# Seven block products in place of eight for two of eight k-pairs of most gate/up column pairs

## The chip, the cores and the metric

The kernel runs on one core of one Trainium2 chip. The metric is the device time of one execution in microseconds (us), and less is better. Before the change the median of three runs is 1765.84 us (1765.79 to 1766.41). Differences within 0.2% of that, some 3.5 us, are treated as no change. All data is fp32 in memory. Each engine works through its own queue of instructions in order and waits at an instruction until the semaphores it names have been reached: TensorE (PE, with its weight loads PEld), VectorE (DVE), ScalarE (ACT), GpSimd (POOL), and SyncE (SP), which here only issues transfers.

## The reference

One decoder layer for 256 tokens of width 2048, with two gated feed-forward networks of inner width 5632 around a mixing layer (linear attention and dilated attention). What is computed, cut to what the change touches:

```
x = x + 0.5 * swiglu(rms_norm(x), w_gate1, w_up1, w_down1)
h = rms_norm(x);  z = h @ w_in;  ... attention ...;  x = x + concat(o_g, o_a) @ w_out
x = x + 0.5 * swiglu(rms_norm(x), w_gate2, w_up2, w_down2)

def swiglu(x, w_gate, w_up, w_down):
    return (silu(x @ w_gate) * (x @ w_up)) @ w_down
```

The change touches `x @ w_gate` and `x @ w_up` in both networks: (256 x 2048) times (2048 x 5632), twice each.

## The kernel before, in words

**Numbers.** TensorE takes its operands as two fp32r parts: a value is split into a high part and the rest. `split` (lines 87 to 90) makes both: ACT copies the source to the high part (line 89), then DVE subtracts it from the source (line 90). A product of two values is then three matmuls: high by high (line 211), high by low part of the weights (line 213), low part of the activations by high (line 215).

**Tiling.** Tokens are two tiles of 128 (`t`). The 2048 input features are 16 k-tiles of 128. The activations of all k-tiles, split, lie in `hh` and `hl`. A gate/up **column pair** is 512 columns of `w_gate` and the same 512 of `w_up`, and there are 11 of them (`b` = 0 to 10) in each network. For one column pair `column_pair` goes through the 16 k-tiles; for each it does both token tiles, both columns and three matmuls of 128x128 by 128x512, that is 12 matmuls, so 192 for a column pair. They accumulate in four PSUM banks `ps` (two token tiles by gate and up).

**Weights.** A `raw` tile holds 1 MB of weights: two k-tiles (a **k-pair**), gate and up. SP loads it (line 181) into one of three buffers; SP can issue the load for a buffer only after the last reader of the tile that lay there before. For each k-tile `prepare` makes a pair of tiles `wh` and `wl` (128x1024) by `split`; each has four buffers (`WBUF`), and ACT can write one only when TensorE has finished with the k-tile four places earlier. `weights` calls `prepare` so that two k-tiles beyond the present one have been asked for.

**Evacuation.** After the last k-tile of a token tile `evac` (lines 263 to 275) applies silu to the gate (ACT, line 265), multiplies by up (DVE, line 266), transposes 32x32 squares (DVE, line 104), moves the squares with 16 small transfers from POOL's queue (line 109) and appends to the list `later` a `finish` that splits the result into `uh` and `ul`, the input of the down projection. `later` is worked off between the k-tiles of the next column pair.

**Order.** The program is written as loops, and a scheduler then sets the order of each engine's queue. PSUM has eight banks: six for accumulators (`pacc`), two for transposes and attention (`ptp`).

Of the kernel before, what the change touches and what calls it, by code (L numbers as in the profile page):

```python
# [26 lines left out]
FT = FF // P  # L27
NT = S // P
EPS = 1e-6
WBUF = 4  # L30
WARM = 10
GH, GDK, GDV, RANK = 4, 128, 256, 16
AH, HD = 8, 128
# [3 lines left out]
def layer_kernel(tc, x, xT, gains, gla_gate_up, gla_gate_bias, gla_out_norm, att_q_norm, att_k_norm,  # L37
# [6 lines left out]
    with ExitStack() as es:  # L44
        cst = es.enter_context(tc.tile_pool(name="cst", bufs=1))
        wp = es.enter_context(tc.tile_pool(name="wp", bufs=2))
        pacc = es.enter_context(tc.tile_pool(name="pacc", bufs=6, space=PSUM))
        ptp = es.enter_context(tc.tile_pool(name="ptp", bufs=2, space=PSUM))

        def acc_bank():  # L50
            return pacc.tile([P, 512], F32, name="acc", tag="acc")

        def t512(name):
            return cst.tile([P, 512], F32, name=name, tag="t512", bufs=4)
# [1 line left out]
        def tp_bank():  # L56
            return ptp.tile([P, 512], F32, name="tp", tag="tp")
# [29 lines left out]
        def split(dst_h, dst_l, src):  # L87

            nc.scalar.activation(dst_h, src, AF.Copy)  # L89
            nc.vector.tensor_sub(dst_l, src, dst_h.bitcast(F32))  # L90
# [20 lines left out]
        def in_order(a):  # L111

            return a.rearrange("p (q j c) -> p j q c", q=4, j=4)

        def runs(a):
            return a.rearrange("p j (q c) -> p j q c", q=4)
# [26 lines left out]
            rsqrt(rt[:, t:t + 1], ssum[:, t:t + 1])  # L143


        jobs = [(w, i, k) for w in (w_ff1, w_dn1) for i in range(w.shape[0]) for k in range(2)]
        jobs += [(w_mix, i, k) for i in range(3 * KT // 2) for k in range(2)] + ["low"]
        jobs += [(w_mix, i, k) for i in range(3 * KT // 2, 3 * KT) for k in range(2)]
        jobs += [(w, i, k) for w in (w_out, w_ff2, w_dn2) for i in range(w.shape[0]) for k in range(2)]

        AHEAD = 2
        ready = []
# [3 lines left out]
        def wtile(name):  # L156
            return wp.tile([P, 2, 512], F32R, name=name, tag=name, bufs=WBUF)

        def prepare():
            if not jobs:  # L160
                return
            job = jobs.pop(0)
            if job == "low":
                raw = wp.tile([P, KT, P], F32, name="raw", tag="raw", bufs=3)
                nc.sync.dma_start(raw, w_low.rearrange("p (k f) -> p k f", f=P))
                got = []
                for i in range(2):
# [7 lines left out]
            if k == 0:  # L175
                raw = raws[0] = wp.tile([P, 2, 2, 512], F32, name="raw", tag="raw", bufs=3)
                flat = raw.rearrange("p k j f -> p (k j f)")
                parts = 1 if started else 4
                started.append(True)
                for c in range(0, 2048, 2048 // parts):  # L180
                    nc.sync.dma_start(flat[:, c:c + 2048 // parts], w[i, :, c:c + 2048 // parts])
            wh, wl = wtile("wh"), wtile("wl")
            if len(started) < 3:
                started.append(True)
                for j in range(2):
                    split(wh[:, j], wl[:, j], raws[0][:, k, j])
            else:
                split(wh, wl, raws[0][:, k])
            ready.append((wh, wl))
# [12 lines left out]
        def halves(a):  # L202
            return a.rearrange("p (b a) -> p b a", b=2)

        def products(ps, t, acts, ws, first, last, js=((0, 1),)):
            for jj in js:
                for i, ((ah, al, k), (wh, wl)) in enumerate(zip(acts, ws)):
                    sh = ah[:, k, t * P:(t + 1) * P]
                    sl = al[:, k, t * P:(t + 1) * P]
                    for j in jj:  # L210
                        nc.tensor.matmul(ps[j], lhsT=sh, rhs=alt(wh[:, j, :]), start=first and i == 0, stop=False)  # L211
                    for j in jj:
                        nc.tensor.matmul(ps[j], lhsT=sh, rhs=alt(wl[:, j, :]), start=False, stop=False)  # L213
                    for j in jj:
                        nc.tensor.matmul(ps[j], lhsT=sl, rhs=alt(wh[:, j, :]), start=False, stop=last and i == len(ws) - 1)  # L215
# [3 lines left out]
        def run_later(n):  # L219
            for _ in range(min(n, len(later))):  # L220
                later.pop(0)()

        def column_pair(acts, evac, span=28, due=None, extra=None, final=False):

            ps = [None] * NT
            n = len(acts)  # L230
            total = done = 0
            i = 0
            while i < n:
                if i == due:
                    done += len(later)
                    run_later(len(later))
                if extra and i in extra:
                    extra[i]()
                g = WBUF if final and i == n - WBUF else 1
                ws = [weights() for _ in range(g)]  # L240
                for t in range(NT):
                    step = 2 * i + t
                    total = max(total, done + len(later))
                    go = max(-(-total * min(step + 1, span) // span) - done, 0)
                    done += min(go, len(later))
                    run_later(go)
                    if i == 0:
                        ps[t] = [acc_bank(), acc_bank()]
                    last = i + g == n
                    products(ps[t], t, acts[i:i + g], ws, i == 0, last, ((0,), (1,)) if g > 1 else ((0, 1),))  # L250
                    if last:
                        evac(t, [b.rearrange("p (a b) -> p b a", b=2) for b in ps[t]])
                i += g
# [3 lines left out]

        def ffn(name, done, extra=None, final=False):
            with tc.tile_pool(name=name, bufs=1, reuse_waits="tile") as fp:
                uh = fp.tile([P, FT, S], F32R, name="uh")  # L260
                ul = fp.tile([P, FT, S], F32R, name="ul")
                for b in range(FF // 512):
                    def evac(t, ps, b=b):
                        sg, u = t512("sg"), t512("u")
                        nc.scalar.activation(halves(sg), ps[0], AF.Silu, scale=rt[:, t:t + 1])  # L265
                        nc.vector.scalar_tensor_tensor(halves(u), ps[1], rt[:, t:t + 1], halves(sg), op0=ALU.mult, op1=ALU.mult)  # L266

                        us = t512("us")
                        ur = fp.tile([P, 512], F32, name="ur", tag="ur", bufs=2)
                        squares(us, u)  # L270
                        move_squares(ur, us)

                        def finish():
                            split(*(runs(a[:, 4 * b:4 * b + 4, t * P:(t + 1) * P]) for a in (uh, ul)), in_order(ur))

                        later.extend([lambda: None] * (2 if t else 6) + [finish])
                    if b:
                        column_pair(hacts, evac)
                    else:
                        column_pair(hacts, evac, span=16, due=15 if extra else 8, extra=extra)  # L280
                for cp in range(2):
                    def evac(t, ps, cp=cp):
                        for j in range(2):
                            c = 2 * cp + j
                            blk = xs[:, t, c * 512:(c + 1) * 512]
                            nc.vector.scalar_tensor_tensor(halves(blk), ps[j], 0.5, halves(blk), op0=ALU.mult, op1=ALU.add)  # L286
                            done(t, c, blk)
                    column_pair([(uh, ul, k) for k in range(FT)], evac, span=28 + 32 * cp, final=final and cp == 1)


        xTv = xT.rearrange("(k p) s -> p k s", p=P)
# [412 lines left out]
```

## Time and profile before

| | |
|---|---|
| median of three runs | 1765.84 us |
| time of the profiled execution | 1764.68 us |
| its span, first to last instruction | 1762.9 us |
| mean granted TensorE clock | 1.000 |
| PE busy | 1753.8 us, 99% of the span, 8244 instructions |
| DVE busy | 998.6 us, 57% |
| ACT busy | 838.1 us, 48% |
| POOL busy | 439.1 us, 25% |
| transfers | 367.57 MB, mean 209 GB/s |

The profile shows one execution. What lies between its span and its time (1.8 us) is start and end. The page groups instructions by source line; "waits" say for which engine's result an engine stood idle; the "chain" follows back from the last instruction what released each step. A wait of an engine that is not the bottleneck costs nothing by itself. The durations of matmuls overlap, so their pace is read from the distance between starts, not from the mean duration.

### The profile page before, as it was taken

The page shows a single profiled execution, that of the slowest core. Times are in us where ns is not written, and L with a number is a line of the kernel's source. Part 1 is how long each engine was busy: PE and PEld are TensorE (multiplying, and loading weights), DVE is VectorE, ACT ScalarE, POOL GpSimd, SP SyncE. Part 2 cuts the span into 40 slices and gives each one's busy share as a digit, 9 for nine tenths or more (in the row PEclk, how much of TensorE's full clock was granted, in tenths as well). Part 3 has the DMA queues.
Part 4 walks back from the last instruction along what each step waited for, and adds up shares of the span by engine and source line. Part 5 has one row for each costly group of instructions (what it writes and reads, how often), then busy time and mean ns, then how long its engine had stood idle before and what let it go on. Part 6 is the DMA issues. An engine that isn't in the chain of part 4 may idle for free. (4 is left out here: it accounts for less than half of the span.)

```text
span 1762.9 us, 21750 instructions
## 1 busy us (share of the span) xinstructions
PE 1753.8 (99%) x8244; PEld 1531.3 (87%) x8244; DVE 998.6 (57%) x1053; ACT 838.1 (48%) x1014; POOL 439.1 (25%) x870
## 2 busy tenths in 40 slices
PE   9999999999999999999999999999999999999999
PEld 8888888888888888888888888888888888888887
DVE  6555555555554656566655656555555555554544
ACT  7444444444444444565654445444444444444442
POOL 0333443434300421011000034333333443410000
PEclk9999999999999999999999999999999999999999
DMA  8666665666655666555444465666656665666653
GB/s 339 223 206 224 207 224 206 221 217 222 212 211 197 223 208 207 210 193 212 155 164 168 154 216 191 217 222 208 223 208 223 208 222 209 216 213 213 217 213 120
DMA packets 80841, 367.57 MB, mean 209 GB/s; under 512 B 19248, under 2 KB 36656, under 8 KB 38496
## 3 DMA queue, kind: packets, MB, share of 16 engines
q1 hardware_dynamic: 50864, 350.25, 56.0%
q0 software_dynamic: 29152, 14.87, 3.3%
q8 instruction: 64, 1.05, 0.2%
q10 hardware_dynamic: 720, 1.07, 0.2%
q14 instruction: 41, 0.34, 0.1%
HBM read 350.38 MB, written 2.10 MB: 200 GB/s over the span
## 5 line engine op out<-in xcount | busy, mean ns | idle before, releaser
L90 DVE TENSOR_TENSOR wl<-raw,wh 128x1024 fp32r<-128x1024 f32 (+1 forms) x658 | 800.0, 1221 | 699.7 <-ACT wh L89 699.0
L89 ACT ACTIVATE wh<-raw 128x1024 fp32r<-128x1024 f32 (+1 forms) x660 | 690.3, 1051 | 854.9 <-PE acc L215 839.7
L213 PE MATMUL acc<-wl,hh 128*128 128x512 f32 x1792 | 547.7, 381 | 0.1
L215 PE MATMUL acc<-wh,hl 128*128 128x512 f32 x1792 | 543.4, 380 | 0.0
L211 PE MATMUL acc<-wh,hh 128*128 128x512 f32 x1792 | 535.6, 381 | 2.1 <-ACT wh L89 1.2
L109 POOL DMA_DIRECT2D ur<-us x704 | 344.4, 497 | 568.0 <-ACT sg L265 428.3
L211 PEld LDWEIGHTS acc<-wh,hh 128*128 128x128 f32 x1792 | 338.1, 189 | 51.3 <-ACT wh L89 2.2
L213 PEld LDWEIGHTS acc<-wl,hh 128*128 128x128 f32 x1792 | 338.2, 189 | 48.8 <-issue 1.0
L215 PEld LDWEIGHTS acc<-wh,hl 128*128 128x128 f32 x1792 | 338.3, 189 | 47.6
L213 PE MATMUL acc<-wl,uh 128*128 128x512 f32 x704 | 212.2, 379 | 0.0
L215 PE MATMUL acc<-wh,ul 128*128 128x512 f32 x704 | 211.8, 379 | 0.0
L211 PE MATMUL acc<-wh,uh 128*128 128x512 f32 x704 | 210.0, 379 | 0.0
L215 PEld LDWEIGHTS acc<-wh,ul 128*128 128x128 f32 x704 | 133.1, 189 | 18.9
L211 PEld LDWEIGHTS acc<-wh,uh 128*128 128x128 f32 x704 | 133.1, 189 | 18.9
L213 PEld LDWEIGHTS acc<-wl,uh 128*128 128x128 f32 x704 | 133.1, 189 | 18.9
L109 POOL DMA_DIRECT2D hh<-us x128 | 62.3, 506 | 174.4 <-issue 136.5
L138 POOL TENSOR_TENSOR rs<-a,mhalf 128x4 f32<-128x4 f32 (+1 forms) x12 | 17.5, 1455 | 257.1 <-DVE a L380 257.1
L266 DVE SCALAR_TENSOR_TENSOR u<-acc,rt,sg 128x512 f32<-128x512 f32 x44 | 32.8, 745 | 0.0
L104 DVE STREAM_TRANSPOSE us<-u 128x512 f32<-128x512 f32 x44 | 31.3, 711 | 1.5
L265 ACT ACTIVATE sg<-acc,rt 128x512 f32<-128x512 f32 x44 | 29.9, 680 | 0.6
L90 DVE TENSOR_TENSOR ul<-ur,uh 128x512 fp32r<-128x512 f32 x44 | 30.1, 684 | 0.0
L89 ACT ACTIVATE uh<-ur 128x512 fp32r<-128x512 f32 x44 | 27.0, 613 | 0.0
(154 smaller groups left out, 573.7 us busy)
## 6 DMA issues: line engine op xcount, KB each, us to landing
raw<-in_w_ff_dram SPq DMA_DIRECT2D x175, 1024.0 KB, 5.0
raw<-in_w_dn_dram SPq DMA_DIRECT2D x88, 1024.0 KB, 4.8
raw<-in_w_mix_dram SPq DMA_DIRECT2D x48, 1024.0 KB, 4.7
raw<-in_w_out_dram SPq DMA_DIRECT2D x16, 1024.0 KB, 4.8
ur<-us POOLq DMA_DIRECT2D x704, 16.0 KB, 3.9
xs<-in_x_dram SPq DMA_DIRECT2D x2, 1024.0 KB, 10.2
hh<-us POOLq DMA_DIRECT2D x128, 16.0 KB, 3.7
xt<-in_xT_dram SPq DMA_DIRECT2D x7, 256.0 KB, 6.5
```

What stands on the lines that cost most here:

```text
L89: nc.scalar.activation(dst_h, src, AF.Copy)
L90: nc.vector.tensor_sub(dst_l, src, dst_h.bitcast(F32))
L104: nc.vector.transpose(dst.rearrange("p (q j c) -> p j q c", q=4, j=4), src)
L109: nc.gpsimd.dma_start(dst[32 * q:32 * q + 32, r * P:(r + 1) * P], src[32 * r:32 * r + 32, q * P:(q + 1) * P])
L138: nc.gpsimd.tensor_tensor(dst, src, mhalf[:, :src.shape[-1]], op=ALU.pow)
L211: nc.tensor.matmul(ps[j], lhsT=sh, rhs=alt(wh[:, j, :]), start=first and i == 0, stop=False)
L213: nc.tensor.matmul(ps[j], lhsT=sh, rhs=alt(wl[:, j, :]), start=False, stop=False)
L215: nc.tensor.matmul(ps[j], lhsT=sl, rhs=alt(wh[:, j, :]), start=False, stop=last and i == len(ws) - 1)
L265: nc.scalar.activation(halves(sg), ps[0], AF.Silu, scale=rt[:, t:t + 1])
L266: nc.vector.scalar_tensor_tensor(halves(u), ps[1], rt[:, t:t + 1], halves(sg), op0=ALU.mult, op1=ALU.mult)
```

## The change

For column pairs `b` = 1 to 7 of both networks (`SEVEN`), the k-pairs 2 and 5 of 0 to 7 (`GROUPS`: k-tiles 4 and 5, and 10 and 11) are multiplied as 2x2 block products in Strassen's manner (Winograd's form): the two token tiles by the two k-tiles, times the two k-tiles by gate and up. Eight block products become seven, each of three matmuls, so 21 matmuls stand where 24 stood. Column pairs 0, 8, 9 and 10, and everything outside gate and up, keep their products.

- **Activations.** `seven_forms` makes four sums or differences of activation blocks for each of the two k-pairs, once for each network, and splits them (`fh`, `fl`).
- **Weights.** A k-pair done so has four jobs in place of two. "plain" (called P here): `raw` holds b11, b12, b21, b22 (k-tile by gate/up); DVE adds b11 to b12 and to b21 (`room["sum"]`, new line 228), and b12, b21 are split to a `wh`/`wl` pair. "last" (L): b22 alone is split into a half-size pair of its own with one buffer (`swh`, `swl`). "sums" (S): two more sums overwrite b21 and b22 in `raw` (line 236, twice), and the two sums of P are split. "more" (M): the two sums in `raw` are split. TensorE uses P for 6 matmuls, L for 3, S for 6 and M for 6.
- **Accumulators.** Three of the seven products go straight into the banks `cs` of the column pair, and four into four banks `ms` of their own, over both k-pairs. So the column pair uses all eight banks (`four_banks`), and the next one uses them the other way round. After the second of these k-pairs `ms` are read into SBUF: one copy (ACT, line 349) and four additions (DVE, lines 350 to 353, "folds"), between the last k-tiles of the column pair.
- **Evacuation.** For each token tile DVE first subtracts a folded sum from the gate (line 409) and adds one to up (line 411); the silu (410) and the multiplication (412) follow.
- **Room.** The last 12 of the 44 tiles of `uh` and `ul` get an allocation of their own, and before it is used the sums and forms lie there. The six accumulator banks become four and two, used in the same turn outside these column pairs.

A column pair done so has 12 k-tiles of 12 matmuls and two groups of 21: 186 matmuls. Its order is k0 to k3, P1 L1 S1 M1, k6 to k9, P2 L2 S2 M2, k12 to k15.

The core of the diff:

```diff
+GROUPS = (2, 5)
+SEVEN = range(1, 8)
+TAIL = FT - 4 * SEVEN[-1] - 4
...
-        pacc = es.enter_context(tc.tile_pool(name="pacc", bufs=6, space=PSUM))
+        pacc = es.enter_context(tc.tile_pool(name="pacc", bufs=4, space=PSUM))
+        paux = es.enter_context(tc.tile_pool(name="paux", bufs=2, space=PSUM))
...
+        def four_banks(odd):
+            if odd:
+                return [paux.tile([P, 512], F32, name="acc", tag="acc") for _ in range(2)] + [tp_bank() for _ in range(2)]
+            return [pacc.tile([P, 512], F32, name="acc", tag="acc") for _ in range(4)]
...
+        def ff_jobs(w):
+            n = KT // 2
+            for i in range(w.shape[0]):
+                if i // n in SEVEN and i % n in GROUPS:
+                    yield from ((w, i, part) for part in ("plain", "last", "sums", "more"))
+                else:
+                    yield from ((w, i, k) for k in range(2))
...
+        def seven(part):
+            raw = raws[0].bitcast(F32)
+            if part == "plain":
+                b1 = raw[:, 0, 0, :].unsqueeze(1).to_broadcast([P, 2, 512])
+                mid = raw.rearrange("p k j f -> p (k j) f")[:, 1:3, :]
+                nc.vector.tensor_add(room["sum"], b1, mid)
+                wh, wl = wtile("wh"), wtile("wl")
+                split(wh, wl, mid)
+            elif part == "last":
+                wh, wl = room["wh"], room["wl"]
+                split(wh[:, 0, :], wl[:, 0, :], raw[:, 1, 1, :])
+            elif part == "sums":
+                for j, b in enumerate((room["sum"][:, 0, :], raw[:, 1, 0, :])):
+                    nc.vector.tensor_add(raw[:, 1, j, :], b, raw[:, 1, j, :])
+                wh, wl = wtile("wh"), wtile("wl")
+                split(wh, wl, room["sum"])
+            else:
+                wh, wl = wtile("wh"), wtile("wl")
+                split(wh, wl, raw[:, 1])
             ready.append((wh, wl))
...
+        def seven_products(cs, ms, kp, first, last):
...
+            def product(bank, a, ws, j, start, stop):
+                nc.tensor.matmul(bank, lhsT=a[0], rhs=alt(ws[0][:, j, :]), start=start, stop=False)
+                nc.tensor.matmul(bank, lhsT=a[0], rhs=alt(ws[1][:, j, :]), start=False, stop=False)
+                nc.tensor.matmul(bank, lhsT=a[1], rhs=alt(ws[0][:, j, :]), start=False, stop=stop)
+            ws = weights()
+            product(ms[0], a11, ws, 0, first, last)
+            product(cs[0], sa, ws, 1, False, False)
+            product(cs[1], a12, weights(), 0, False, False)
+            ws = weights()
+            product(ms[1], s1, ws, 0, first, last)
+            product(ms[3], s3, ws, 1, first, last)
+            ws = weights()
+            product(ms[2], s2, ws, 0, first, last)
+            product(cs[3], a22, ws, 1, False, False)
...
+                    nat = [m.rearrange("p (a b) -> p b a", b=2) for m in ms]
+                    p1, u, u2, u3 = [halves(a) for a in room["rest"]]
+                    folds = [lambda: nc.scalar.activation(p1, nat[0], AF.Copy),
+                             lambda: nc.vector.tensor_add(u, p1, nat[2]),
+                             lambda: nc.vector.tensor_add(u2, u, nat[3]),
+                             lambda: nc.vector.tensor_add(u, u, nat[1]),
+                             lambda: nc.vector.tensor_add(u3, u2, nat[1])]
...
+                        if rest:
+                            nc.vector.tensor_sub(halves(sg), ps[0], rest[0])
+                            nc.scalar.activation(sg, sg, AF.Silu, scale=rt[:, t:t + 1])
+                            nc.vector.tensor_add(rest[1], ps[1], rest[1])
+                            nc.vector.scalar_tensor_tensor(halves(u), rest[1], rt[:, t:t + 1], halves(sg), op0=ALU.mult, op1=ALU.mult)
```

**Where the order moves.** The numbers in the rows below are the scheduler's names of tiles. First place: DVE's queue at the end of a column pair. Before, from the last two k-tiles (`raw_750`) through the first k-pair of the next column pair to its second:

```order
L90 TENSOR_TENSOR wl_753<-raw_750,wh_752 128x1024
L90 TENSOR_TENSOR ul_123<-ur_488,uh_122 128x4x128
L90 TENSOR_TENSOR wl_769<-raw_750,wh_768 128x1024
L90 TENSOR_TENSOR wl_835<-raw_832,wh_834 128x1024
L266 SCALAR_TENSOR_TENSOR u_779<-acc_513,rt_75,sg_778 128x512
L104 STREAM_TRANSPOSE us_782<-u_779 128x4x4x32
L90 TENSOR_TENSOR wl_855<-raw_832,wh_854 128x1024
L266 SCALAR_TENSOR_TENSOR u_810<-acc_521,rt_75,sg_809 128x512
L104 STREAM_TRANSPOSE us_813<-u_810 128x4x4x32
L90 TENSOR_TENSOR wl_873<-raw_870,wh_872 128x1024
```

And now, from the last k-tile (k15, `raw_1457`) over k0 and k1 (`raw_1495`) to k2 (`raw_1586`):

```order
L105 TENSOR_TENSOR wl_1478<-raw_1457,wh_1477 128x1024
L352 TENSOR_TENSOR t4_512<-t4_512,acc_1303 128x512
L353 TENSOR_TENSOR t4_512<-t4_512,acc_1303 128x512
L105 TENSOR_TENSOR wl_1498<-raw_1495,wh_1497 128x1024
L105 TENSOR_TENSOR wl_1517<-raw_1495,wh_1516 128x1024
L105 TENSOR_TENSOR swl_514<-raw_1620,swh_513 128x512
L105 TENSOR_TENSOR ul_126<-ur_1213,uh_125 128x4x128
L409 TENSOR_TENSOR sg_1532<-acc_1231,t4_512 128x512
L411 TENSOR_TENSOR t4_512<-acc_1232,t4_512 128x512
L105 TENSOR_TENSOR wl_1589<-raw_1586,wh_1588 128x1024
L411 TENSOR_TENSOR t4_512<-tp_1234,t4_512 128x512
L412 SCALAR_TENSOR_TENSOR u_1533<-t4_512,rt_78,sg_1532 128x512
```

Half-size tile L1 of the next column pair (`swl` from `raw_1620`) has moved ahead of the evacuation of the old one. `raw_1620` takes the buffer of `raw_1457`, three tiles earlier.

Second place: the same queue a little later. Before, the k-tiles stand there in a row:

```order
L90 TENSOR_TENSOR wl_889<-raw_870,wh_888 128x1024
L90 TENSOR_TENSOR wl_907<-raw_904,wh_906 128x1024
L90 TENSOR_TENSOR wl_923<-raw_904,wh_922 128x1024
L90 TENSOR_TENSOR wl_941<-raw_938,wh_940 128x1024
L90 TENSOR_TENSOR wl_957<-raw_938,wh_956 128x1024
```

And now from S1 and M1 (`raw_1620`) over k6 to k9 (`raw_1676`, `raw_1698`) to group 2 (`raw_1732`):

```order
L228 TENSOR_TENSOR t4_512<-raw_1620 128x1024
L236 TENSOR_TENSOR raw_1620<-t4_512,raw_1620 128x512
L236 TENSOR_TENSOR raw_1620<-raw_1620 128x512
L105 TENSOR_TENSOR wl_1660<-t4_512,wh_1659 128x1024
L105 TENSOR_TENSOR wl_1670<-raw_1620,wh_1669 128x1024
L105 TENSOR_TENSOR wl_1679<-raw_1676,wh_1678 128x1024
L105 TENSOR_TENSOR wl_1689<-raw_1676,wh_1688 128x1024
L105 TENSOR_TENSOR wl_1701<-raw_1698,wh_1700 128x1024
L228 TENSOR_TENSOR t4_512<-raw_1732 128x1024
L105 TENSOR_TENSOR wl_1717<-raw_1698,wh_1716 128x1024
L105 TENSOR_TENSOR swl_514<-raw_1732,swh_513 128x512
L105 TENSOR_TENSOR wl_1736<-raw_1732,wh_1735 128x1024
```

The additions for group 2 (`raw_1732`, in the buffer of `raw_1620`) stand ahead of the `wl` of k9.

TensorE's queue at this place. Before, one k-tile after another:

```order
L211 MATMUL acc_838<-wh_906,hh_68 128x512
L211 MATMUL acc_839<-wh_906,hh_68 128x512
L213 MATMUL acc_838<-wl_907,hh_68 128x512
L213 MATMUL acc_839<-wl_907,hh_68 128x512
L215 MATMUL acc_838<-wh_906,hl_69 128x512
L215 MATMUL acc_839<-wh_906,hl_69 128x512
```

And now S1 (`wh_1659`), M1 (`wh_1669`) and k6 (`wh_1678`):

```order
L288 MATMUL acc_1654<-wh_1659,fh_515 128x512
L288 MATMUL tp_1656<-wh_1659,fh_515 128x512
L288 MATMUL tp_1655<-wh_1669,fh_515 128x512
L288 MATMUL acc_1585<-wh_1669,hh_71 128x512
L289 MATMUL acc_1654<-wl_1660,fh_515 128x512
L290 MATMUL acc_1654<-wh_1659,fl_516 128x512
L289 MATMUL tp_1656<-wl_1660,fh_515 128x512
L290 MATMUL tp_1656<-wh_1659,fl_516 128x512
L264 MATMUL acc_1582<-wh_1678,hh_71 128x512
```

In group 1 the matmuls with the high part of M1 now stand right behind those of S1, ahead of the low part of S1.

Third place: ACT's queue at the end of the column pair. Before:

```order
L89 ACTIVATE wh_768<-raw_750 128x1024
L89 ACTIVATE wh_834<-raw_832 128x1024
L265 ACTIVATE sg_778<-acc_512,rt_75 128x512
L89 ACTIVATE wh_854<-raw_832 128x1024
L265 ACTIVATE sg_809<-acc_520,rt_75 128x512
```

And now:

```order
L104 ACTIVATE wh_1516<-raw_1495 128x1024
L104 ACTIVATE swh_513<-raw_1620 128x512
L104 ACTIVATE uh_125<-ur_1213 128x4x128
L104 ACTIVATE wh_1588<-raw_1586 128x1024
L410 ACTIVATE sg_1532<-sg_1532,rt_78 128x512
L104 ACTIVATE wh_1604<-raw_1586 128x1024
```

Here too the half-size tile of the next column pair (`swh` from `raw_1620`) stands ahead of the silu.

More of the change, by code (lines that the diff above doesn't have):

```diff
@@ L174, in prepare @@
             w, i, k = job
-            if k == 0:
+            if k in ("last", "sums", "more"):
+                return seven(k)
+            if k == "plain" or k == 0:
                 raw = raws[0] = wp.tile([P, 2, 2, 512], F32, name="raw", tag="raw", bufs=3)
@@ L188, in prepare @@
                 split(wh, wl, raws[0][:, k])
+            ready.append((wh, wl))
+        room = {}
+        def seven(part):
[17 more added lines that the diff above has]
+                split(wh, wl, raw[:, 1])
             ready.append((wh, wl))
@@ new lines, in seven_pair @@
+        def seven_pair(b, evac):
+            cs = four_banks(b % 2)
+            ms = None
+            folds = []
+            order[0] = 4 * (1 - b % 2)
+            units = []
+            for kp in range(KT // 2):
+                units += [kp] if kp in GROUPS else [(2 * kp,), (2 * kp + 1,)]
+            total = done = 0
+            steps = 2 * (len(units) - len(GROUPS))
+            step = 0
+            for n, unit in enumerate(units):
+                if isinstance(unit, tuple):
+                    ws = [weights()]
+                    for t in range(NT):
+                        step += 1
+                        total = max(total, done + len(later))
+                        go = min(max(-(-total * step // steps) - done, 0), len(later))
+                        done += go
+                        run_later(go)
+                        if folds:
+                            folds.pop(0)()
+                        products([cs[2 * t], cs[2 * t + 1]], t, [hacts[unit[0]]], ws, n == 0, n == len(units) - 1)
+                    continue
+                if ms is None:
+                    ms = four_banks(1 - b % 2)
+                last = unit == GROUPS[-1]
+                seven_products(cs, ms, unit, unit == GROUPS[0], last)
+                if last:
+                    nat = [m.rearrange("p (a b) -> p b a", b=2) for m in ms]
[5 more added lines that the diff above has]
+                             lambda: nc.vector.tensor_add(u3, u2, nat[1])]
+            for t in range(NT):
+                rest = ((u, p1), (u3, u2))[t]
+                evac(t, [c.rearrange("p (a b) -> p b a", b=2) for c in cs[2 * t:2 * t + 2]], rest)
@@ L273, in finish @@
                         def finish():
-                            split(*(runs(a[:, 4 * b:4 * b + 4, t * P:(t + 1) * P]) for a in (uh, ul)), in_order(ur))
+                            uh, ul, k = part(4 * b)
+                            split(*(runs(a[:, k:k + 4, t * P:(t + 1) * P]) for a in (uh, ul)), in_order(ur))
                         later.extend([lambda: None] * (2 if t else 6) + [finish])
-                    if b:
+                    if b == SEVEN[0]:
+                        sp = rooms.enter_context(tc.tile_pool(name=name + "s", bufs=1, reuse_waits="tile"))
+                        t4 = sp.tile([P, 4, 512], F32, name="t4")
+                        room["rest"] = [t4[:, i, :] for i in range(4)]
+                        room["sum"] = t4[:, 2:4, :]
+                        for n in ("wh", "wl"):
+                            room[n] = sp.tile([P, 1, 512], F32R, name="s" + n)
+                        for n in ("fh", "fl"):
+                            f = sp.tile([P, len(GROUPS), 4, P], F32R, name=n)
+                            room[n] = {kp: f[:, g] for g, kp in enumerate(GROUPS)}
+                        later[:0] = [lambda kp=kp: seven_forms(kp) for kp in GROUPS]
+                    elif b == SEVEN[-1] + 1:
+                        rooms.close()
+                        rp = rooms.enter_context(tc.tile_pool(name=name + "t", bufs=1, reuse_waits="tile"))
+                        us_h.append(rp.tile([P, TAIL, S], F32R, name="uh2"))
+                        us_l.append(rp.tile([P, TAIL, S], F32R, name="ul2"))
+                    if b in SEVEN:
+                        seven_pair(b, evac)
+                    elif b:
                         column_pair(hacts, evac)
@@ L287, in evac @@
                             done(t, c, blk)
-                    column_pair([(uh, ul, k) for k in range(FT)], evac, span=28 + 32 * cp, final=final and cp == 1)
+                    column_pair([part(k) for k in range(FT)], evac, span=28 + 32 * cp, final=final and cp == 1)
+                rooms.close()
         xTv = xT.rearrange("(k p) s -> p k s", p=P)
```

46 lines of the change are left out of this document (38 added, 8 removed).

## The prediction

> **What bounds the kernel now.** I read the page's busy times first, then the waits, the chain of waits, and the timeline of one column pair.
>
> ```profile
> PE 1753.8 (99%) x8244; PEld 1531.3 (87%) x8244; DVE 998.6 (57%) x1053; ACT 838.1 (48%) x1014; POOL 439.1 (25%) x870
> ...
> ACT wh L89 <- PE acc L215: 839.7, 571, 4.8
> DVE wl L90 <- ACT wh L89: 699.0, 537, 3.7
> ...
> PE acc L211 <- ACT wh L89: 1.2, 2, 0.8
> ```
>
> TensorE is busy 99% and waits for weights twice, 1.2 us in all. ACT waits 839.7 us for TensorE to give weight buffers back, and DVE waits for ACT. So the number of matmuls sets the time. The chain gives their pace, by the same three matmuls of each column pair:
>
> ```profile
> 1160.52 0.65 PE acc L211 x3
> ...
> 1533.47 0.65 PE acc L211 x3
> ```
>
> Nine column pairs in 372.95 us are 41.44 each; by 192 matmuls, 0.2158 us per matmul.
>
> **What the change removes.** 2 groups x 7 column pairs x 2 networks = 28 groups, each 3 matmuls fewer: 84 x 0.2158 = **18.1 us**. A changed column pair has 186 matmuls, 40.14 us. The new products write one bank three times running; the profile has such a run at the end of the kernel, at the same pace:
>
> ```profile
> 1756.05 0.38 PE L211 MATMUL acc<-wh,uh 128*128 128x512 f32 x1
> 1756.27 0.38 PE L213 MATMUL acc<-wl,uh 128*128 128x512 f32 x1
> 1756.48 0.38 PE L215 MATMUL acc<-wh,ul 128*128 128x512 f32 x1
> ```
>
> **What it adds to DVE.** The groups of instructions by shape, and the busy time in the 42 us around one column pair (PE, PEld, DVE, ACT, POOL):
>
> ```profile
> L90 DVE TENSOR_TENSOR wl<-raw,wh 128x1024 fp32r<-128x1024 f32 x654 | 797.3, 1224 | 694.9 <-ACT wh L89 694.2
> L266 DVE SCALAR_TENSOR_TENSOR u<-acc,rt,sg 128x512 f32<-128x512 f32 x44 | 32.8, 745 | 0.0
> L90 DVE TENSOR_TENSOR ul<-ur,uh 128x512 fp32r<-128x512 f32 x44 | 30.1, 684 | 0.0
> L90 DVE TENSOR_TENSOR hl<-hf,hh 128x512 fp32r<-128x512 f32 x16 | 10.8, 682 | 0.7 <-ACT hh L89 0.7
> L286 DVE SCALAR_TENSOR_TENSOR xs<-acc,xs 128x512 f32<-128x512 f32 x16 | 10.3, 682 | 10.2 <-PE acc L215 10.2
> L620 DVE TENSOR_TENSOR xs<-xs,acc 128x512 f32<-128x512 f32 x8 | 5.2, 677 | 2.7 <-PE acc L215 2.7
> ...
> 215.00:257.00 42.00, 42.00 (x196) 36.79 (x195) 23.99 (x23) 19.33 (x21) 15.65 (x32) 1.00 0.62 217
> ```
>
> An addition of 1024 columns costs 1.22 us, one of 512 0.68, from SBUF (L90) or PSUM (L620, L286) alike. Per changed column pair: for each group one of 1024 (L228), two of 512 (L236), and splits of 3 x 1024 + 512 in place of 2 x 1024, 1.22 + 1.37 + 1.91 = 4.5; four folds 2.7; four additions in the evacuation 2.7. That is 9.0 + 5.4 = 14.4 us on top of 24.0, 38.4 of DVE in 40.1 us of TensorE. It nearly fits; whether it fits depends on the order and on what DVE must wait for. ACT goes from 19.3 to about 24 us and has room.
>
> **The ring.** Back-to-back instructions of DVE overlap a little, so I need the distances between starts:
>
> ```profile
> 5.03 0.69 DVE L90 TENSOR_TENSOR wl<-raw,wh 128x512 fp32r<-128x512 f32 x1 [3.59 <-ACT wh L89]
> 5.64 0.88 DVE L304 SCALAR_TENSOR_TENSOR hl<-xt,gT,hh 128x256 fp32r<-128x256 f32 x2
> ...
> 213.45 1.06 ACT L89 ACTIVATE wh<-raw 128x1024 fp32r<-128x1024 f32 x1 [1.53 <-PE acc L215]
> ...
> 214.54 1.23 DVE L90 TENSOR_TENSOR wl<-raw,wh 128x1024 fp32r<-128x1024 f32 x1 [1.36 <-ACT wh L89]
> 215.69 0.75 DVE L266 SCALAR_TENSOR_TENSOR u<-acc,rt,sg 128x512 f32<-128x512 f32 x1
> 216.47 0.71 DVE L104 STREAM_TRANSPOSE us<-u 128x512 f32<-128x512 f32 x1
> 217.13 1.23 DVE L90 TENSOR_TENSOR wl<-raw,wh 128x1024 fp32r<-128x1024 f32 x1
> ...
> L89 ACT ACTIVATE uh<-ur 128x512 fp32r<-128x512 f32 x44 | 27.0, 613 | 0.0
> ```
>
> A 1024 subtraction takes 1.15 to the next start, one of 512 0.61, a transpose 0.66; L266 takes 0.78 where the next needs its result (0.03 after its end) and so, by the same overlap, about 0.66 otherwise. ACT's result is taken up 0.03 later. There are three `raw` buffers, and by the order the one of k14/k15 goes to group 1 of the next column pair, then to its group 2, then to its k14/k15. DVE reads each of them last, and stands still for two of the loads. That closes a ring that TensorE isn't in. Transfers to landing, in 5 us windows from 202, 207, 212, 217, 227, and over 100 us from 1200:
>
> ```profile
> DMA to landing us min/median/max: 4.7/4.7/4.7
> DMA to landing us min/median/max: 4.8/4.8/4.8
> DMA to landing us min/median/max: 5.1/5.1/5.1
> DMA to landing us min/median/max: 5.6/5.6/5.6
> DMA to landing us min/median/max: 5.3/5.3/5.3
> DMA to landing us min/median/max: 4.7/5.1/6.7
> ```
>
> They are 4.7 to 4.8 in quiet stretches and 5.1 to 5.6 while POOL moves squares (217 to 234). The ring, from the end of k15's `wl`:
> - `raw` of group 1 lands: 4.75 + 0.05 for hand-over = 4.80 (quiet).
> - ACT makes `swh`, and nothing of the evacuation passes it on either queue: 0.61 + 0.03 = 0.64.
> - DVE from `swl` through `wl` of M1: seven of 512 (`swl`, `ul`, L409 twice, L411 twice, the second L236) 4.24; four of 1024 (k2, k3, P1, S1) 4.60; L412 0.66 and 0.78; two transposes 1.32; L228 and the first L236 with results needed at once 1.25 + 0.72; `wl` of M1 to its end 1.27. Sum 14.84.
> - `raw` of group 2 lands, amid the squares: 5.3 + 0.05 = 5.35.
> - DVE from L228 through k15's `wl`: L228, k9, P2, S2 4.60; `swl` and L236 1.21; second L236, then ACT's 1.06 for M2, 1.80; M2, k12 2.30; k13 1.37 (ACT has the fold's copy ahead of it); L350 and L351 1.21; k14 1.15; k15 to its end 1.23. Sum 14.87.
>
> Behind `swh` on ACT stand `uh`, the `wh` of k2 and the silu of the evacuation; behind `swl` on DVE the whole evacuation, which could begin 1 us sooner (L409 stands at 39.8, TensorE is done with token tile 0 at 38.9). Behind L228 of group 2 stands the `wl` of k9, which comes at 61.1 from the column pair's start and is due at 63.2. On SP the load of k6/k7 stands behind that of group 1 and isn't due for 15 us.
>
> **Ring: 4.80 + 0.64 + 14.84 + 5.35 + 14.87 = 40.5 us against 40.14** of TensorE. So each column pair DVE falls 0.36 us further behind, until TensorE waits.
>
> How much it may fall behind: in the first changed column pair k15's `wl` isn't late. L350 needs the fourth matmul of M2, which starts 29.14 us after the column pair and takes 0.38; then L350, k14, L351 and k15 take 0.61 + 1.15 + 0.61 + 1.23: end at 33.1. M1's high part is ready after 0.64 + 4.80, then 11.81 to the second L236, 0.69 of it, 0.03 and 1.06 of ACT: 19.0 later, at 52.15. TensorE needs it two matmuls into S1, at 40.14 + 12.73 = 52.87. **Slack 0.72 us**; S1's low part has 1.1. Five ring turns lie between column pairs 1 and 7, so a network loses 5 x 0.36 - 0.72 = 1.1 us, both 2.2. Each halt costs a restart: after one, four matmuls take 1.13 in place of 0.38 + 3 x 0.216 = 1.03, so 0.1 in three column pairs of each network, 0.6.
>
> ```profile
> 13.32 1.13 PE L211 MATMUL acc<-wh,hh 128*128 128x512 f32 x4 [0.83 <-ACT wh L89]
> ...
> 13.30 2.36 DVE L90 TENSOR_TENSOR wl<-raw,wh 128x1024 fp32r<-128x1024 f32 x2 [1.98 <-ACT wh L89]
> ...
> 1099.48 1.23 DVE L90 TENSOR_TENSOR wl<-raw,wh 128x1024 fp32r<-128x1024 f32 x1 [0.77 <-ACT wh L89]
> ```
>
> **The forms** cost DVE, for each of two k-pairs in each network, 0.68 + 0.68 and four of 128 columns (no row; below 0.48, the L304 of 256 above): under 3.3 us, four times, 13 us were nothing to hide them. At the start DVE idles 1.98 us just there; in network 2 it has caught up at 1099.48. Both lie in column pair 0, where weights are made ahead. I take 0.3 (0 to 3).
>
> **PSUM.** `cs` of a column pair are the `ms` of the one before, read 5 us earlier; `ms` are the old `cs`, needed 10 us later. Price nothing; were the folds late, the next column pair's first matmul would wait.
>
> **Sum:** -18.1 + 2.2 + 0.6 + 0.3 = -15.0, against the profiled execution 1764.7 - 15.0 = 1749.7. The median of the runs is 1.2 us above it: **1751 us**.
>
> The ring's bounds. Lower: transfers at 4.7 and 5.1, ring 40.2, nothing lost. Upper: the six PSUM readers in it (L350, L351, L409, L411) at L266's 745 ns, +0.4, and transfers of 5.6 and 6.7, +2.2: 43.1, a loss of 2 x (5 x 2.96 - 0.72) = 28 us. L228 has no row; it is nearest to `wl`, the same operands and size.
>
> [...] L620 and L286 read PSUM in 677 and 682 ns, `hl` reads SBUF in 682. [...]
>
> **The rivals.**
> - *It fits.* Ring at or under 40.28 (5 x 0.14 = 0.72): 1766 - 18.1 + 0.3 = 1748. For it: 0.2 us in 40 is less than my rounding, and landing at 4.7 was seen. Against: each hand-over not listed only lengthens the ring. Chance 27%.
> - *PSUM reads dearer.* The six readers at 745 ns: ring 40.9, loss 2 x (3.8 - 0.7) = 6.2 and 1 us of restarts, 1755. L266, which has two operators and a scalar more, speaks for it, L620 and L286 against: 4%. With other lengthenings of the kind (landings of 5.6, which by themselves make 41.7 and 1763), 1754 to 1761: 14%. [...]
> - *DVE becomes the bound.* Place: the ring's `raw` buffer. From a ring of 42.1 on the waits (2 x (5 x 1.96 - 0.72) = 18.2) eat the gain; at the upper bound 1751 - 2 + 28 = 1777, slower. For it: 38.4 us of DVE in 40.1, and two transfers in series with it. Against: the landings would both have to be the slowest seen. 14% beyond 1761, 8% of them slower.
>
> **How the numbers follow.** Forecast 45% (1748.8 to 1754), fits 27%, dearer 14%, bound 14%. Range 1747 to 1761: the floor without loss, less the scatter of the runs, to where the third rival begins; it leaves 14%, and a little below. A measurement can tell 0.2%, 3.5 us, from no change: faster (under 1762.3) 0.86, same 0.06, slower 0.08.
>
> **What would show it.** PE 84 instructions fewer; column pairs 1 to 3 of each network 40.1 us apart, 5 to 7 about 40.5; TensorE's waits at S1 or M1 of group 1 (lines 288, 289), on ACT or DVE, growing from column pair to column pair, none in group 2; DVE waiting for `raw` at L228 of group 2, ACT at `swh`. Wrong if waits stand at k0 of a column pair (folds late), in column pair 0 (forms), or if the matmuls' pace isn't 0.216.

## The result, and the profile after

The changed kernel takes 1749.99 us in the median of four runs (1748.53 to 1750.96), the kernel before 1765.82 on the same chip (1764.57 to 1766.41): a ratio of 0.9911 (95% interval 0.9895 to 0.9926), 15.8 us less. A later series gave 0.9912 (0.9898 to 0.9927). The forecast was 1751 us with a range of 1747 to 1761. The profiled execution took 1748.53 us, 16.15 less than that of before; the forecast for it was 1749.7.

The busy times on the page of the changed kernel, then its waits:

```profile
PE 1736.6 (99%) x8160; PEld 1515.7 (87%) x8160; DVE 1179.1 (68%) x1329; ACT 885.2 (51%) x1088; POOL 438.4 (25%) x870
```

```profile
PE acc L264 <- ACT wh L104: 2.0, 2, 1.2
...
PE tp L288 <- ACT wh L104: 0.3, 1, 0.3
PE acc L288 <- ACT wh L104: 0.2, 1, 0.2
...
ACT swh L104 <- DMA raw<-in_w_ff_dram: 55.2, 27, 2.9
...
DVE t L228 <- DMA raw<-in_w_ff_dram: 23.6, 14, 1.9
...
DVE swl L105 <- ACT swh L104: 20.9, 12, 2.3
```

There are 84 matmuls fewer, as forecast. DVE went from 57 to 68% and now waits for `raw` at line 228 once in each changed column pair (14 times), and for `swh`, which itself waits for a transfer. TensorE shows only two short waits in the new products (line 288); its two waits at line 264 are at the start of network 1 (at 7.51 and 13.55 us). The chain of waits, in order of time (start, us, what), shows more. Now it leaves TensorE from column pair 4 to 6 of network 1:

```profile
205.12 4.79 DMA raw<-in_w_ff_dram
209.93 0.64 ACT swh L104
...
220.35 1.12 DVE t L228
...
224.11 1.24 DVE wl L105
225.36 5.06 DMA raw<-in_w_ff_dram
230.45 1.23 DVE t L228
...
244.15 1.15 DVE wl L105
245.31 5.26 DMA raw<-in_w_ff_dram
250.60 0.64 ACT swh L104
...
263.69 1.07 ACT wh L104
```

This is the ring of the prediction, link by link: transfer, `swh`, DVE, transfer, DVE, and the next transfer starts 40.19 us after the first (245.31 - 205.12). At 263.69 ACT begins M1's high part, and TensorE waits for it until 264.80.

What TensorE loses is read from the starts of the products of L, the only ones that use `swh`. From TensorE's timeline, groups 1 and 2 of column pairs 3 and 6, and the one wait:

```profile
142.26 0.38 PE L288 MATMUL acc<-swh,hh 128*128 128x512 f32 x1
157.15 0.38 PE L288 MATMUL acc<-swh,hh 128*128 128x512 f32 x1
...
263.30 0.38 PE L288 MATMUL acc<-swh,hh 128*128 128x512 f32 x1
264.80 0.48 PE L288 MATMUL tp<-wh,fh 128*128 128x512 f32 x1 [0.25 <-ACT wh L104]
278.72 0.38 PE L288 MATMUL acc<-swh,hh 128*128 128x512 f32 x1
```

From group 1 to group 2 it takes 14.89 us undisturbed, which is 69 matmuls at 0.2158, and 15.42 in column pair 6. The wait in brackets is 0.25, the loss 0.53: distances between starts show all of it, the list of waits not. All changed column pairs read in this way (us over 14.89; the way from group 2 to the next group 1 is 25.25 or 25.26 everywhere):

| column pair | 1 | 2 | 3 | 4 | 5 | 6 | 7 | sum |
|---|---|---|---|---|---|---|---|---|
| network 1 | 0 | 0 | 0 | 0.38 | 0.23 | 0.53 | 0 | 1.14 |
| network 2 | 0 | 0 | 0 | 0.01 | 0.49 | 0.09 | 0.27 | 0.86 |

Together 2.00 us, all in group 1, none before column pair 4. 18.13 - 2.00 = 16.13, against 16.15 measured.

### The profile page after: what moved, and what is told of

It is laid out like the page before. It is cut to its first block, busy times and chain, and to the rows that moved or that the text cites. A ratio compares the mean times of both kernels' runs of the same rounds, so it can differ in the third digit from the quotient of the medians.

```text
span 1746.8 us, 21964 instructions
## 1 busy us (share of the span) xinstructions
PE 1736.6 (99%) x8160; PEld 1515.7 (87%) x8160; DVE 1179.1 (68%) x1329; ACT 885.2 (51%) x1088; POOL 438.4 (25%) x870
## 3 DMA queue, kind: packets, MB, share of 16 engines
q0 software_dynamic: 29152, 14.87, 3.3%
## 4 chain that ended last, share of the span: by engine, by line
PE 90%; DMA 4%; DVE 4%; issue 1%; ACT 1%; POOL 1%; DVEq 0%; SPq 0%; ACTq 0%; POOLq 0%
PE acc L266 25%; PE acc L268 25%; PE acc L264 25%; PE tp L264 2%; PE tp L266 2%; PE tp L268 2%; DMA raw<-in_w_ff_dram 2%; DVE wl L105 2%; PE acc L290 1%; PE acc L289 1%; PE acc L288 1%; DMA hh<-us 1%; DMA ur<-us 1%; PE tp L100 1%; ACT wh L104 1%
## 5 line engine op out<-in xcount | busy, mean ns | idle before, releaser
L266 PE MATMUL acc<-wl,hh 128*128 128x512 f32 x1376 | 416.8, 381 | 0.1
L268 PE MATMUL acc<-wh,hl 128*128 128x512 f32 x1376 | 414.9, 381 | 0.0
L264 PE MATMUL acc<-wh,hh 128*128 128x512 f32 x1376 | 409.1, 381 | 2.0 <-ACT wh L104 2.0
L264 PEld LDWEIGHTS acc<-wh,hh 128*128 128x128 f32 x1376 | 259.7, 189 | 39.3 <-ACT wh L104 2.7
L266 PEld LDWEIGHTS acc<-wl,hh 128*128 128x128 f32 x1376 | 259.6, 189 | 37.7 <-issue 1.0
L268 PEld LDWEIGHTS acc<-wh,hl 128*128 128x128 f32 x1376 | 259.8, 189 | 36.4 <-DVE hl L473 0.2
L264 PE MATMUL tp<-wh,hh 128*128 128x512 f32 x192 | 58.5, 379 | 0.0
L266 PE MATMUL tp<-wl,hh 128*128 128x512 f32 x192 | 57.1, 379 | 0.0
L268 PE MATMUL tp<-wh,hl 128*128 128x512 f32 x192 | 57.1, 379 | 0.0
L228 DVE TENSOR_TENSOR t<-raw 128x1024 f32<-128x1024 f32 x28 | 33.8, 1207 | 23.6 <-DMA raw<-in_w_ff_dram 23.6
```

The lines of the kernel that those rows point to most:

```text
L228: nc.vector.tensor_add(room["sum"], b1, mid)
```

## The experiments

The rivals for the 2.0 us are the ring (two transfers in series with DVE), the mere amount of DVE's work, and the order of S1 and M1. "Lengthening" below is the sum of such a table.

### More work in the ring

```diff
             elif part == "sums":
+                nc.vector.tensor_add(junk, room["sum"][:, 0, :], room["sum"][:, 1, :])
```

> One more addition of 512 columns on VectorE in each changed group, after the sums of P are made and before S is split (its result is used nowhere). The ring theory: each addition takes 0.61 us to the next start and both lie in the ring. The new order also puts the second addition of S behind a split in group 1, some 0.6 us, and moves the additions of group 2 behind the split of k9. I make the ring 41.8 us against 40.14 of TensorE; five turns in each network, less a slack of 0.5: a loss of 2 x (5 x 1.7 - 0.5) = 16 us in place of the 2.0 that the changed kernel shows, so its profiled execution at about 1762 us (1758 to 1766), the column pairs from 3 on 41.8 us apart, all of the lengthening in group 1. The rival that VectorE has room as long as its work fits (37.7 us busy of 40.14, and 1.2 more make 38.9): no wait of TensorE beyond those there are, 1748.5 us.

1764.41 us in the median (1761.69 to 1768.39), ratio to before 0.9991 (0.9981 to 1.0): 19 us of DVE time (28 additions of 687 ns), with the new order that they bring, took back the gain, to within what the runs can tell. The profiled execution took 1765.48, at the upper end of what the ring gives. The waits of TensorE, and the products of L in group 1 of column pairs 3 and 7 of network 1:

```profile
PE acc L289 <- ACT wh L104: 4.1, 7, 0.8
...
PE tp L289 <- ACT wh L104: 2.1, 4, 0.6
```

```profile
143.52 0.38 PE L289 MATMUL acc<-swh,hh 128*128 128x512 f32 x1
...
310.59 0.38 PE L289 MATMUL acc<-swh,hh 128*128 128x512 f32 x1
```

(310.59 - 143.52) / 4 = 41.77 us to a column pair, and 42.1 in network 2; 41.8 was forecast for the ring. Single column pairs from there on took 41.2 to 43.5. The lengthening is 18.1 us, against 16 forecast. That DVE has room as long as its work fits is refuted for these positions.

### The first group one k-pair later

```diff
-GROUPS = (2, 5)
+GROUPS = (3, 5)
```

> The same change with the first group one k-pair later: k-pairs 3 and 5 in place of 2 and 5. The work of every engine is the same. The ring theory: the buffer of a raw tile is that of three tiles before. With the groups at 3 and 5 the evacuation or a group stands on VectorE between the last read of that tile and the first use of the new one at every place (5.35 us ahead of the half-size tile of group 1, 6.0 ahead of the additions of group 2, against 4.8 and 5.3 for the transfers), so VectorE waits for no transfer, its turn is its work of some 38 us, and TensorE loses nothing in the changed column pairs: all 40.14 apart, 2.0 us less than the changed kernel, profiled execution about 1746.5 us, median about 1748. The rival that the 2.0 us come from VectorE's work as such, or from something else in group 1 (its order of S1 and M1, the two forms of activations): the lengthening stays, 1748.5.

1748.52 us (1747.04 to 1748.98), ratio 0.9902 (0.9888 to 0.9917). By time alone this can't be told from the changed kernel, and the profiled execution took 1748.92, not the 1746.5 forecast: outside the changed column pairs its halts are 0.7 us longer in all (4.61 against 3.88), and a half clock cost an estimated 1.7 (last section), which eats the 2.0. Inside them the profile tells the two apart. The waits of TensorE, all there are, and DVE's for a transfer at line 228:

```profile
PE acc L264 <- ACT wh L104: 2.7, 1, 2.7
PE tp L100 <- DVE hf L114: 1.9, 1, 1.9
PE tp L93 <- DVE warm L90: 1.5, 1, 1.5
...
DVE t L228 <- DMA raw<-in_w_ff_dram: 1.3, 3, 0.5
```

None of TensorE's is in a changed column pair (they are at the start and ahead of network 2). DVE's waits at line 228 fell from 23.6 us in 14 to 1.3 in 3, all in column pair 1. The seven column pairs follow each other at 40.14 or 40.15 us in both networks: lengthening 0 in place of 2.0. Work and instructions are those of the changed kernel. The order in group 1 is not: in 12 of 14 groups of the changed kernel the high part of M1 stood ahead of the low part of S1, and here S1's products come first in all. So this run does not separate the ring from the order of S1 and M1; the run with a buffer of its own does.

### Both together

> The added 512-column additions of the first run together with the groups at k-pairs 3 and 5. The ring theory: no transfer is in the chain, VectorE's work is 37.7 + 1.2 = 38.9 us in 40.14, so the additions cost nothing: 1746.5 us in the profiled execution as without them, up to 1748 for waits on ScalarE behind the sums. The rival that added work on VectorE costs what it lasts wherever the groups are: 1758 us or more, as in the first run.

The edits of the last two kernels in one. 1747.13 us (1746.78 to 1748.2), ratio 0.9897 (0.9882 to 0.9912); profiled execution 1746.78, 1746.5 forecast. All changed column pairs are 40.14 or 40.15 apart. With the additions the two positions are 17.3 us apart (1764.41 - 1747.13), without them 1.5 (1749.99 - 1748.52): the additions cost 14.4 us at 2 and 5 (1764.41 - 1749.99) and nothing at 3 and 5. One column pair of each, from L of group 1 to the next (stretch, busy PE, PEld, DVE, ACT, POOL, clock, DMA share, GB/s), that of "More work in the ring" first:

```profile
185.56:227.36 41.80, 40.91 (x188) 34.91 (x187) 37.18 (x44) 22.04 (x25) 15.78 (x33) 1.00 0.60 214
```

```profile
228.30:268.44 40.14, 40.14 (x187) 35.15 (x186) 37.00 (x43) 22.89 (x26) 15.60 (x33) 1.00 0.64 223
```

DVE is busy 37.18 and 37.00 us; the turn is 41.80 and 40.14. So it is not the amount of DVE's work but the transfers in series with it.

### One group only

```diff
-GROUPS = (2, 5)
+GROUPS = (2,)
```

> Only k-pair 2 is multiplied with seven products, 42 matmuls more than the changed kernel. By the pace of 0.2158 us per matmul 9.06 us more, and no ring loss (VectorE has 4.5 us less to do in each column pair), 2.0 us less: profiled execution 1755.6 us, changed column pairs 40.79 us apart without exception. If each group also costs something beyond its matmuls (restarts, forms), the 9.06 would be smaller.

The column pairs are 40.79 or 40.80 us apart, as forecast, but the time is 1761.49 us in the median of seven runs (1756.27 to 1762.69). The two runs with a full clock took 1756.27 and 1757.25; the five others, granted 0.997 or 0.998, 1760.25 to 1762.69. The profiled execution is the slowest, 7.1 above the 1755.6 forecast; the two runs with a full clock are 0.7 and 1.7 above it. The rest is told in the last section. Group 1 has the changed kernel's order of S1 and M1 here, again in 12 of 14, and none is late.

### Three groups

```diff
-GROUPS = (2, 5)
+GROUPS = (1, 3, 5)
```

> Three of the eight k-pairs (1, 3 and 5) with seven products: 42 matmuls fewer than the changed kernel, 9.06 us, and a column pair of 39.49 us. A third group adds to VectorE, start to start, one addition of 1024 columns, two of 512, one split of 1024 and one of 512: 1.14 + 1.30 + 1.14 + 0.60 = 4.2 us, so 41.9 in place of 37.7. VectorE is then the bound whatever the buffers do: 2.4 us too much in each of five or six turns, 2 x (5 x 2.4 - 0.5) = 23 to 28 us lost, up to 10 more if it also waits for transfers. From the 1746.5 us without a ring loss: 1760 to 1775 in the profiled execution, near or above the kernel before the change, waits of TensorE in most changed column pairs. The rival that VectorE has room for it: 1737.5.

1795.93 us (1793.74 to 1798.43), ratio 1.0177 (1.016 to 1.0194): slower than before the change with 126 matmuls fewer, and 20 us beyond what I expected. Waits of this kernel, and busy times (stretch, PE, PEld, DVE, ACT, POOL, clock, DMA share, GB/s) in the second and the sixth turn of network 1, from L to L of its first group:

```profile
PE acc L288 <- ACT wh L104: 26.1, 18, 2.5
```

```profile
DVE t L228 <- DMA raw<-in_w_ff_dram: 25.9, 14, 3.0
```

```profile
96.35:140.28 43.93, 40.69 (x184) 34.11 (x183) 39.18 (x45) 23.41 (x27) 14.70 (x31) 1.00 0.58 203
...
272.54:316.76 44.22, 41.64 (x184) 35.59 (x183) 40.10 (x47) 23.76 (x27) 15.92 (x33) 0.96 0.56 203
```

DVE is busy 39.18 and 40.10 us of these turns, about TensorE's 39.49 and less than the 41.9 forecast, but the turns last 43.93 and 44.22: it waits for one transfer in each column pair (25.9 us in 14) and for ACT. From the second column pair on, the mean is (316.76 - 96.35) / 5 = 44.1 us, 4.6 over TensorE's. With the halts inside the last column pair that is about six turns in each network, 12 x 4.6 = 55 us, and 1737.5 + 55 = 1792.5 agrees with the profiled 1793.74. I had put in the work alone, 2.4 over, and left the waits out. TensorE stands idle for some 32 us of the 55 at lines 288 and 289, and the clock of 0.991 over 1792.0 us is an estimated 16 more; it follows the halts. How DVE's waits divide between transfers, ACT and POOL's moves of squares, through which the chain of waits runs in the fifth turn, these runs don't settle.

### A buffer of its own for group 2

```diff
-                raw = raws[0] = wp.tile([P, 2, 2, 512], F32, name="raw", tag="raw", bufs=3)
+                if k == "plain" and i % (KT // 2) == GROUPS[1]:
+                    raw = raws[0] = room["pool"].tile([P, 2, 2, 512], F32, name="raw", tag="own", bufs=1)
+                else:
+                    raw = raws[0] = wp.tile([P, 2, 2, 512], F32, name="raw", tag="raw", bufs=3)
...
-                            f = sp.tile([P, len(GROUPS), 4, P], F32R, name=n)
+                            f = sp.tile([P, 1, 4, P], F32R, name=n)
```

> The changed kernel with its groups at k-pairs 2 and 5 and a fourth raw buffer that only the second group uses; the other weights go round the three as before. To make room, both groups use one set of activation forms (that of k-pair 5), so the products of k-pair 2 are formed with the wrong sums; every instruction, size and transfer stays. The ring theory: the transfer of group 2 no longer follows the last split of group 1. What is left of the ring is 4.84 + 0.66 + 14.75 + 17.6 = 37.9 us, under 40.14: no lengthening of any column pair, no wait of VectorE for raw at line 231, profiled execution 1746.5 us, median 1748. The rival that the loss comes from the order of group 1 or from VectorE's work: the column pairs 4 to 7 stay 0.1 to 0.5 us longer, 1748.5.

To make room, both groups use the sums of activations of k-pair 5, so this kernel leaves out those of k-pair 2 and does not compute the layer; instructions, sizes and transfers stay. 1747.52 us (1746.39 to 1750.85), ratio 0.9901 (0.9887 to 0.9916). The profiled execution took 1748.44, which by time alone is the rival's 1748.5; a half clock after a halt at its start is in it (last section). DVE no longer appears as waiting for a transfer at line 231 (the 228 of before). Column pair 6 of network 1, which was lengthened most, takes 14.89 again:

```profile
264.88 0.38 PE L291 MATMUL acc<-swh,hh 128*128 128x512 f32 x1
279.77 0.38 PE L291 MATMUL acc<-swh,hh 128*128 128x512 f32 x1
```

The lengthening is 0.3 us in all, 0.27 of it in one column pair, where a `wl` of k6 comes late behind the additions of group 2. Positions and the order of S1 and M1 (12 of 14 groups) are those of the changed kernel, so neither of these alone is the cause: one buffer more opens the ring. The scheduler moved the additions of group 2 forward as well, so the buffer was not the only thing that changed.

### One column pair more, and the changed kernel again

```diff
-GROUPS = (2, 5)
-SEVEN = range(1, 8)
+GROUPS = (3, 5)
+SEVEN = range(1, 9)
...
+                if i % (KT // 2) == GROUPS[0]:
+                    room["half"] = room["pool"].tile([P, 2, 512], F32R, name="two", tag="two")
+                wh, wl = room["half"][:, 0:1, :], room["half"][:, 1:2, :]
...
+                    two = room["pool"].tile([P, 2, 512], F32, name="two", tag="two")
+                    p1, u, u2, u3 = [halves(a[:, i, :]) for a in (two, room["sum"]) for i in range(2)]
```

> Groups at k-pairs 3 and 5, and column pair 8 changed as well (1 to 8): 12 matmuls fewer, 2.6 us. Since the last 8 tiles of the split results in place of 12 now have to hold the sums and forms, the half-size tile shares its room with the first two folded sums. The ring theory: VectorE's turn is its work, under 40.14 us, so all changed column pairs are 40.14 us apart, and the profiled execution takes about 1744 us, the median about 1746. If the shared room makes the half-size tile late (it now waits for the evacuation of token tile 0), TensorE halts at the products of L in group 1, and the gain goes.

> The changed kernel as it is, once more, on the same chip as the three others, to set them against it: 1748.5 us in the profiled execution, 1750 in the median, lengthened column pairs 4 to 7 with about 2 us in all.

The wider kernel takes 1745.66 us (1743.58 to 1746.31), ratio 0.9886 (0.9871 to 0.9900), profiled execution 1743.58; the changed kernel beside it 1750.04 (1749.63 to 1750.40), ratio 0.9912. The two sets of runs don't overlap. The page of the wider one, and its products of L in group 1 of column pairs 1 and 8 of network 1:

```profile
PE 1732.7 (99%) x8148; PEld 1513.3 (87%) x8148; DVE 1206.6 (69%) x1365; ACT 902.6 (52%) x1098; POOL 438.5 (25%) x870
```

```profile
67.47 0.38 PE L290 MATMUL acc<-two,hh 128*128 128x512 f32 x1
...
348.48 0.38 PE L290 MATMUL acc<-two,hh 128*128 128x512 f32 x1
```

(348.48 - 67.47) / 7 = 40.14: no lengthening in eight column pairs, and the shared room makes nothing late for TensorE (ACT waits for it 14 times, 15.3 us in all). It is faster than the changed kernel and the one before. The changed kernel showed its lengthening again, 1.65 us (0.29 and 0.81 in column pairs 4 and 6 of network 1, 0.55 in 5 of network 2).

## Why the prediction was right, step by step

**The matmuls.** 84 fewer at 0.2158 us, 18.1 us: undisturbed column pairs are 40.14 apart, and 40.79 with one group. Exact.

**The ring.** The forecast was 40.5 us. `swh` of group 1 starts in column pairs 2 and 7 of network 1 at

```profile
88.26 0.63 ACT L104 ACTIVATE swh<-raw 128x512 fp32r<-128x512 f32 x1 [1.72 <-DMA raw<-in_w_ff_dram]
...
290.65 0.63 ACT L104 ACTIVATE swh<-raw 128x512 fp32r<-128x512 f32 x1 [2.26 <-DMA raw<-in_w_ff_dram]
```

so a turn took (290.65 - 88.26) / 5 = 40.48 us, and 40.41 in network 2. In the turn of the chain above, by its links: first transfer to its landing 4.81 (forecast 4.80), `swh` through M1's `wl` 15.43 (15.48), second transfer 5.09 (5.35), line 228 through k15 14.86 (14.87). In this turn three links are right to 0.05. Over the ten turns from column pair 2 to 7 of both networks DVE's two stretches stay within 0.03 of these figures, and all the rest is transfers: the first took 4.67 to 5.31 with its hand-over, 4.98 in the mean, the second 4.94 to 5.30, mean 5.16. So the first was put 0.18 too short, since single ones took up to 5.31, and the second 0.19 too long; that these cancel to 40.5 is luck. Single turns lay between 40.05 and 40.92, so TensorE's halts come and go; they don't grow from pair to pair as the forecast had it, and column pair 7 of network 1 lost nothing. DVE's work was put too high as well: its busy time is 35.84 us from L to L of column pair 4 of network 1 (182.41 to 222.93) against 38.4, in part because durations were added where its instructions overlap (1.22 us for 1024 columns, 1.15 to the next start). The ring went by distances between starts and did not carry that over.

**The slack and the restarts.** Five turns exceed 40.14 by 1.7 us in all in network 1 and 1.3 in network 2; the losses are 1.14 and 0.86, so the slack was about 0.5, not 0.72. The term that failed is the 0.6 us for restarts as an addition: the 2.00 us read from the starts already hold them, so the ring and its restarts cost 2.0 where the sum had 2.8. Most of the 1.2 us between forecast and profiled execution is this: a restart delays TensorE (four matmuls at 13.55, after the halt of 1.24, took 1.13 us in place of 1.03), but the ring, which TensorE isn't in, sets when the next weights come. That reading is argued; no run takes the restarts apart.

**The forms.** 0.3 us forecast. The first matmul of the down projection in network 1 stands in the timelines of before and of after at

```profile
464.48 0.59 PE L211 MATMUL acc<-wh,uh 128*128 128x512 f32 x2
```

```profile
456.78 0.60 PE L264 MATMUL acc<-wh,uh 128*128 128x512 f32 x2
```

so it comes 7.70 us sooner, which is 9.06 less 1.14 less 0.22; column pair 1 starts 0.23 later than before. By the same reading at later places the mixing part gained 0.5 and the start of network 2 lost 0.3. The start of network 1 moves with TensorE's halts for its first weights as well (0.83 us before; 0.74 and 1.24 after), so the forms' own price is not told apart from these few tenths.

**PSUM.** The rival that its readers are dearer is out. The groups of DVE's instructions by shape:

```profile
L236 DVE TENSOR_TENSOR raw<-t,raw 128x512 f32<-128x512 f32 x28 | 19.4, 692 | 0.9
...
L411 DVE TENSOR_TENSOR t<-acc,t 128x512 f32<-128x512 f32 x20 | 13.7, 683 | 0.0
L409 DVE TENSOR_TENSOR sg<-acc,t 128x512 f32<-128x512 f32 x20 | 13.5, 676 | 1.5 <-PE acc L268 1.5
```

Reading PSUM takes 676 and 683 ns, SBUF alone 692: no price of a PSUM source shows in these forms.

**DVE as the bound.** This rival lay 1.6 us of ring away: the first experiment made it 41.8 and the gain was gone (the forecast gave 42.1 for no gain left), and the third group made the kernel slower than before.

**The places.** All of the loss is in group 1 and none before column pair 4, none at k0, and the waits of DVE and ACT for `raw` are at line 228 and at `swh`, as forecast.

## What to carry to other kernels

Where an in-order engine is the last reader of a rotating buffer and then waits for the transfer into it, its work and the transfer add up (30.29 us from `swh` and line 228 through the last `wl`, and 9.90 of transfers, in the turn of 40.19 here): count the turn of the buffers, not the engine's busy share (68% of the span here, 35.84 of 40.52 us in a changed column pair). Such a ring is opened by moving a block of that engine's other work between the last read and the next first use, or by one more buffer: the lengthening, 2.00 us here, went to 0 by the first and to 0.3 by the second. Read losses from distances between starts of the same instruction, since the list of waits showed 0.5 of 2.0 us.

## What the hardware showed that I had not expected

After some short halts of TensorE the granted clock fell to half for a few microseconds. The kernel with one group, in stretches after a halt of 2.73 us at its start (stretch, PE busy, clock, DMA share, GB/s):

```profile
14.80:16.00 1.20, 1.13 (x4) 1.00 1.11 445
16.00:18.00 2.00, 1.91 (x5) 0.53 0.96 391
18.00:20.00 2.00, 2.00 (x7) 0.62 1.11 404
20.00:22.00 2.00, 2.00 (x11) 1.00 0.96 389
```

and the changed kernel in its later series, right after a halt of 2.08:

```profile
14.00:16.00 2.00, 2.00 (x5) 0.50 1.06 423
16.00:18.00 2.00, 2.00 (x8) 0.65 0.98 394
18.00:20.00 2.00, 2.00 (x11) 1.00 1.08 415
```

5 to 8 matmuls stand in 2 us there in place of 11. The kernel with one group had a second such stretch, which began within a halt of 3.75 us ahead of network 2, and its clock over the whole execution is 0.997. The granted clock in its trace is 0.50 from 16.11 to 19.53 and from 1087.90 to 1094.72, that is 3.41 and 6.83 us; half of 3.41, an estimated 1.7 us, is lost beside the halt itself. By their windows the stretches of the two fences above add up to the same: (2.00 x 0.47 + 2.00 x 0.38) / 0.5 and (2.00 x 0.50 + 2.00 x 0.35) / 0.5 are both 3.4 us. Halts of 1.81 and 1.93 us were enough in two profiles (the kernel with a buffer of its own, at its start, and the one with the first group later, ahead of network 2), and halts of 1.81 to 1.83 (three profiles), 1.90, 2.38 and 2.68 passed without it, so the length of the halt alone does not decide. Five such stretches of the kernel with three groups, in network 2, begin 44.37 us apart each time (1181.05 to 1358.54), while the turns there took 44.1 to 44.8. What sets that distance, and what decides beside the length of a halt, is not shown. Halts of 1.25 us and less never had it, the kernel with three groups left aside. All of these lie at the start and ahead of network 2, outside the changed column pairs. They fit the way the runs of the kernel with one group divide by their clocks (one of them was profiled), and are one reason, not shown to be the only one, why runs of the others differ by about as much as the whole ring loss: the changed kernel's profiled execution had clock 1.000, its three other runs 0.999 and 1.3 to 2.4 us more.
